# PEER with gathered rows: 1.3 rows per step in front of and during the first range's weights, and fewer chunks of U made early

## The chip, the cores and the metric

One core of a Trainium2 chip. The metric is the device time of one execution in microseconds (us). TensorE (PE) multiplies matrices, VectorE (DVE), ScalarE (ACT) and GpSimd (POOL) work on rows of 128 partitions, SyncE (SP) issues most transfers. Each engine runs its own instructions strictly in the order in which the program has them, and waits by semaphores for the others.

## The reference

Two models run one after the other. The part that the change touches is layer 0 of the first model, where the same PEER layer is applied to two streams of 256 tokens of width 1024, the context xc and the latents x:

```python
def _peer(h, w_q, keys, u_tab, v_tab):
    def block(hb):
        ...
        e = i1 * N_KEYS + i2
        g = jax.nn.softmax(sc.astype(jnp.float32), axis=-1).astype(hb.dtype)
        a = jax.nn.gelu(jnp.einsum('nhkd,nd->nhk', u_tab[e], hb)) * g
        return jnp.einsum('nhk,nhkd->nd', a, v_tab[e])
...
        x = x + mod[5] * _peer(h, *peer_args)
        if not last:
            ...
            xc = xc + modc[5] * _peer(hc, *peer_args)
```

Each token chooses 8 x 16 = 128 of 16384 experts. For each chosen expert e, row e of U is dotted with the token, gelu is applied, the result is weighted by g, and row e of V times that number is added.

## The kernel before

`peer0` computes the layer for both streams at once, in two different ways.

*The context is gathered.* `gathered` is a generator that yields after each row. A "row" here is a tile of 128 x 1024 f32, 512 KB, which POOL fetches with one indirect DMA (`rows_of`, L1394): for one token its 128 rows of V, or for 128 tokens one row of U each. First come 256 rows of U; VectorE dots each with the tokens (L1409, into `dots`). After each 128, gelu and weights follow. Then come 256 rows of V, one for each token; TensorE multiplies each with eight small products into `ps_gv`. After every 32 rows ScalarE copies the result (`yg`, L1435), TensorE transposes it (`ps_gT`), and VectorE adds it to the stream's state `XC` (L1443, L1444). The buffers for rows are four quarters of one tile `gb`, and two more (`ht`) once U's rows are done.

*The latents are dense.* All 16384 experts are computed in 128 chunks of 128. `first()` (L1476) loads one chunk of U (512 KB), multiplies (`ps_U`, f32) and puts gelu of it (L1481) into a ring `A` of 52 chunks. `peer_weights` (L1218) makes the factors g of 32 experts' chunks (a range) in 33 steps: VectorE makes P (L1244), P (L1247) and Pg (L1250), TensorE multiplies them (`ps_G`, f16), and `use` (L1232) multiplies the ring's chunks with the result. `second(c)` (L1483) splits the ring's chunk into a high and a low part (`a_hi` L363 on ACT, `a_lo` L364 on DVE), loads a chunk of V, splits that too (`whi` L350, `wlo` L353) and adds twelve products to `ps_acc`. After chunk 127 `peer_out` copies `ps_acc` to `y`, transposes it (`ps_yT`) and adds it to X (L1571). The next stage begins with the sums of squares of XC and X (`sq` L523 and L540, POOL's additions `R` L527, `ps_ss`), the reciprocal `R` (L555) and the projection `ps_in`.

*What sets the order.* `units(n)` (L1470) adds n to a credit and takes one row from the generator for each whole credit. It is called in the front of the context (`fc`), in the front of x (`fx`, 46 steps), once per `first()` in the steps of range 1's weights (`gens[0]`), and then with 2.1 (`UNITS`) after each `second` and each `first`. Rows that are left when the loop ends are taken at its end, before the stage closes. `first()` is called in the fronts under a condition on the step's number; what the ring of 52 then lacks (`more`) is spread over the 33 steps of the first range. A scheduler reorders instructions within what dependences and buffers allow, so that an instruction's place on its engine can be ahead of its place in the program.

Of the kernel before, what the change touches and what calls it, by code (L numbers as in the profile page):

```python
# [297 lines left out]
class Kern:  # L298
# [1153 lines left out]
    def peer0(self, side=()):  # L1452


        nc = self.nc
        es = ExitStack()
        self.ctx_done = False
        self.peer_open(es, 1, self.RANGES0)
        pe = self.pe
        self.keys = pe.tile([P, 2, P], FT, name="keys")  # L1460
        nc.sync.dma_start(self.keys, self.A["keys0"].rearrange("p (q e) -> p q e", q=2))
        sc, sx = {}, {}
        self.gather_open(sc)
        R = self.RING0
        A = pe.tile([P, R, NT], FT, name="A")
        pos = {"u": 0, "v": 0}
        credit = [0.0]
        gath = self.gathered(sc)

        def units(n=None):  # L1470
            credit[0] += self.UNITS if n is None else n
            while credit[0] >= 1 and not self.ctx_done:
                next(gath)
                credit[0] -= 1

        def first():  # L1476
            c = pos["u"]
            pos["u"] += 1
            ps = self.psb("ps_U")[:, :NT]
            self.lin_32(self.load_w(self.A["U0"][c]), sx["h"], ps)  # L1480
            nc.scalar.activation(A[:, c % R], ps, AF.Gelu_apprx_tanh)  # L1481

        def second(c):  # L1483
            t = A[:, c % R]
            a = (pe.tile([P, NT], FR, tag="a_hi", bufs=2, name="a_hi"),
                 pe.tile([P, NT], FR, tag="a_lo", bufs=2, name="a_lo"))
            self.hilo(a[0], a[1], t)
            w = self.weight(self.A["V0"][c])
            for b in range(2):
                bs = slice(b * P, (b + 1) * P)  # L1490
                for n in range(2):
                    ns = slice(n * 512, (n + 1) * 512)
                    self.mm3(acc[2 * b + n], (a[0][:, bs], a[1][:, bs]), (w[0][:, ns], w[1][:, ns]), c == 0, c == P - 1)

        def ahead():
            return pos["u"] < P and pos["u"] < pos["v"] + R and sx.get("h") is not None

        fc, fx = self.peer_front(0, 0, sc, True), self.peer_front(0, 1, sx)
        self.pool_each = 1 << 30
        next(fc)  # L1500
        while "h" not in sx:
            next(fx)
            next(fc)
        for k, _ in enumerate(fc):
            if (k > 24 or k % 4 == 3) and ahead():
                first()
            if "blocks" in sc:
                units(1)
        for k, _ in enumerate(fx):
            if (k > 32 or k % 2) and ahead():  # L1510
                first()
            units(self.UNITS / 2)
        ranges, i0 = [], 0
        for n in self.RANGES0:
            ranges.append((i0, n))
            i0 += n
        gens = [self.peer_weights(sx, A, i0 % R, i0, n) for i0, n in ranges]
        side = [f(pe) for f in side]
        NB = NT // self.TB + 1
        more = R - pos["u"]  # L1520
        for k, _ in enumerate(gens[0]):
            for _ in range((k + 1) * more // NB - k * more // NB):
                first()
                units()
        nr, left = 1, NB
        for c in range(P):
            pos["v"] = c
            if c == 0:
                acc = [self.psa("ps_acc") for _ in range(4)]
            if nr < len(ranges):  # L1530
                i0, n = ranges[nr]
                if pos["u"] >= i0 + n:
                    k = -(-left // max(1, i0 - c - 1))
                    for _ in range(min(k, left)):
                        next(gens[nr])
                        left -= 1
                    if left == 0:
                        nr, left = nr + 1, NB
            second(c)
            units()  # L1540
            pos["v"] = c + 1
            if ahead():
                first()
                units()
            if not self.ctx_done:
                self.advance(side)
            if c == P - 1:
                self.peer_out(0, 1, acc)
        for _ in gath:
            pass  # L1550
        self.advance(side, 1000)
        self.pool_each = 4
        es.close()
# [803 lines left out]
```

## Time and profile before

| | |
|---|---|
| median of 3 runs | 4083.49 us (4080.9 to 4084.05) |
| profiled execution | 4071.07 us |
| its span | 4069.2 us |
| granted TensorE clock, mean | 0.961 of full speed |
| TensorE busy | 3736.2 us (92%) |
| VectorE busy | 2718.9 us (67%) |
| ScalarE, GpSimd busy | 1522.1 us, 1333.6 us |
| U rows dotted (L1409) | 256 x 1.22 us |

The stage of `peer0` that matters here lies between 867 and 1984 us of the span. The table of stretches below gives, for each stretch, its length, then for each engine the busy time with the number of instructions in brackets, the granted clock of TensorE (1.00 is full speed, 0.50 half), the busy share of the 16 DMA engines and the GB/s they moved. Timeline rows have the start, the duration of a run of like instructions, the engine, the line, the operation, out<-in, and in square brackets the idle time of the engine before them with what ended it. A tile's view lists how long and how often the engine of an instruction on that tile stood idle before it, by what ended that.

### The profile page before, as it was taken

To read this page: it belongs to the slowest core of one execution; us is meant where nothing else is said; L and a number is where in the kernel's file an instruction comes from. 1 tells how busy PE (TensorE), PEld (TensorE's weight loads), DVE (VectorE), ACT (ScalarE), POOL (GpSimd) and SP (SyncE) were. 2 spreads that over 40 slices of the span, in tenths; PEclk is the share of its full clock that TensorE was granted. 3 is DMA by queue.
4 is the path that set the end of the run, shared out by engine and by line. 5 is a ranking of instruction groups with operands and counts; after the bars stand their busy time and mean duration, and the time that the engine had idled before them with its cause. 6 is when DMAs were issued, how large, how long until landed. Compare 5 with 4: busy or idle time off the path is not lost. (4 is left out here: it accounts for less than half of the span.)

```text
span 4069.2 us, 69007 instructions
## 1 busy us (share of the span) xinstructions
PE 3736.2 (92%) x26811; PEld 3164.7 (78%) x26811; DVE 2718.9 (67%) x5739; ACT 1522.1 (37%) x2552; POOL 1333.6 (33%) x916
## 2 busy tenths in 40 slices
PE   8999996866898889999799988999999999999999
PEld 6777875755676666666589988889778899999999
DVE  5833368788787642374585799886785666864785
ACT  6433320111121211233455443444334646553554
POOL 0022205432435434455314456322442131231122
PEclk9999997987898999999899999999999999999999
DMA  5254238965989889999545544556446413565355
GB/s 211 70 166 140 79 119 281 334 218 192 355 306 365 333 312 354 336 353 403 194 130 163 160 146 126 160 168 191 150 146 189 144 48 113 178 198 179 92 178 151
DMA packets 228952, 827.48 MB, mean 203 GB/s; under 512 B 25736, under 2 KB 27408, under 8 KB 228624
## 3 DMA queue, kind: packets, MB, share of 16 engines
q1 hardware_dynamic: 154752, 554.08, 42.2%
q0 software_dynamic: 73728, 268.47, 17.8%
q8 instruction: 211, 3.46, 0.3%
q14 instruction: 117, 0.96, 0.1%
q10 hardware_dynamic: 144, 0.52, 0.0%
HBM read 821.91 MB, written 1.06 MB: 202 GB/s over the span
## 5 line engine op out<-in xcount | busy, mean ns | idle before, releaser
L350 ACT CAST whi<-raw 128x1024 fp32r<-128x1024 f32 (+1 forms) x774 | 802.0, 1039 | 975.8 <-DMA raw<-in_V 322.0
L353 POOL TENSOR_TENSOR wlo<-raw,whi 128x1024 fp32r<-128x1024 f32 (+1 forms) x230 | 570.6, 2482 | 1457.8 <-ACT whi L350 1308.5
L353 DVE TENSOR_TENSOR wlo<-raw,whi 128x1024 fp32r<-128x1024 f32 (+1 forms) x544 | 670.2, 1233 | 459.8 <-ACT whi L350 454.6
L1394 POOL DMA_INDIRECT gb<-in_Ur,er x256 | 329.6, 1288 | 536.0 <-DVE gb L1409 300.3
L323 PE MATMUL ps_U<-h,raw 128*128 128x256 f32 x2048 | 483.1, 392 | 23.9 <-ACT A L1481 23.7
L323 PEld LDWEIGHTS ps_U<-h,raw 128*128 128x128 f32 x2048 | 398.5, 197 | 93.7 <-ACT A L1481 24.6
L323 PE MATMUL ps_acc<-wlo,a_hi 128*128 128x512 f32 x1024 | 420.6, 411 | 46.2 <-DVE wlo L353 43.7
L323 PE MATMUL ps_acc<-whi,a_hi 128*128 128x512 f32 x1024 | 430.2, 424 | 15.4 <-ACT whi L350 15.4
L323 PE MATMUL ps_acc<-whi,a_lo 128*128 128x512 f32 x1024 | 415.7, 406 | 0.0
L1409 DVE SCALAR_TENSOR_TENSOR gb<-gb,ht 128x1024 f32<-128x1024 f32 x256 | 310.2, 1223 | 124.3 <-DMA gb<-in_Ur,er 123.1
L363 ACT CAST a_hi<-A 128x256 fp32r<-128x256 f32 x256 | 103.5, 405 | 568.4 <-PE ps_acc L323 525.5
L323 PE MATMUL ps_U<-h_hi,whi 128*128 128x256 f32 x1024 | 294.3, 287 | 7.9 <-DVE A L1232 5.4
L323 PE MATMUL ps_U<-h_hi,wlo 128*128 128x256 f32 x1024 | 291.4, 285 | 8.4 <-DVE wlo L353 6.5
L323 PE MATMUL ps_U<-h_lo,whi 128*128 128x256 f32 x1024 | 290.8, 284 | 0.0
L323 PEld LDWEIGHTS ps_acc<-wlo,a_hi 128*128 128x128 f32 x1024 | 200.5, 196 | 95.3 <-DVE wlo L353 53.3
L323 PE MATMUL ps_in<-hh_hi,whi 128*128 128x256 f32 (+1 forms) x776 | 265.9, 345 | 1.7 <-ACT hh_hi L568 1.7
L323 PE MATMUL ps_in<-hh_hi,wlo 128*128 128x256 f32 (+1 forms) x776 | 262.3, 339 | 1.1 <-POOL wlo L353 1.1
L323 PEld LDWEIGHTS ps_acc<-whi,a_hi 128*128 128x128 f32 x1024 | 198.6, 195 | 83.0 <-ACT whi L350 20.7
L323 PE MATMUL ps_in<-hh_lo,whi 128*128 128x256 f32 (+1 forms) x776 | 262.9, 340 | 0.0
L364 DVE TENSOR_TENSOR a_lo<-A,a_hi 128x256 fp32r<-128x256 f32 x256 | 117.5, 460 | 201.8 <-ACT a_hi L363 199.7
L1394 POOL DMA_INDIRECT gb<-in_V,eT x170 | 182.5, 1073 | 178.0 <-PE ps_gv L323 145.4
L323 PEld LDWEIGHTS ps_acc<-whi,a_lo 128*128 128x128 f32 x1024 | 200.6, 196 | 47.6 <-DVE a_lo L364 0.6
(636 smaller groups left out, 8748.9 us busy)
## 6 DMA issues: line engine op xcount, KB each, us to landing
raw<-in_U SPq DMA_DIRECT2D x256, 512.0 KB, 4.3
raw<-in_V SPq DMA_DIRECT2D x256, 512.0 KB, 4.5
raw<-in_win SPq DMA_DIRECT2D x96, 512.0 KB, 3.8
raw<-in_wup SPq DMA_DIRECT2D x88, 512.0 KB, 3.8
raw<-in_wada SPq DMA_DIRECT2D x80, 512.0 KB, 4.8
raw<-in_wq SPq DMA_DIRECT2D x48, 512.0 KB, 4.5
raw<-in_gwin SPq DMA_DIRECT2D x37, 512.0 KB, 3.7
raw<-in_wdn SPq DMA_DIRECT2D x32, 512.0 KB, 4.1
```

Of the source, the lines that this page charges most:

```text
L323: self.nc.tensor.matmul(o, l, r, start=start, stop=stop)
L350: nc.scalar.copy(hi[:, :f], raw[:, :f])
L353: eng.tensor_sub(lo[:, :f], raw[:, :f], hi[:, :f].bitcast(FT))
L363: (copy or self.nc.scalar.copy)(hi, src)
L364: self.nc.vector.tensor_sub(lo, src, hi.bitcast(FT))
L1394: self.nc.gpsimd.indirect_dma_start(t, None, table, bass.IndirectOffsetOnAxis(ap=at, axis=0), bounds_check=P * P - 1, oob_is_err=False)
L1409: nc.vector.scalar_tensor_tensor(t, t, 1.0, st["ht"][:, b], op0=OP.mult, op1=OP.mult, accum_out=st["d"][:, b, j:j + 1])
```

## The change

Two loops of `peer0` are changed, three lines in all.

```diff
         for k, _ in enumerate(fx):
-            if (k > 32 or k % 2) and ahead():
+            if k % 2 and ahead():
                 first()
-            units(self.UNITS / 2)
+            units(1.3)
...
         for k, _ in enumerate(gens[0]):
             for _ in range((k + 1) * more // NB - k * more // NB):
                 first()
-                units()
+            units(1.3)
```

In the front of x, `first()` is called at odd steps alone, where before it was called at every step after the 32nd; 23 chunks of U are made there instead of 29, 44 in both fronts instead of 50, and 8 of the ring's 52 instead of 2 are left for range 1's weights. The credit is 1.3 per step there instead of 1.05. In the 33 steps of range 1's weights it is 1.3 per step, in place of 2.1 per chunk of U. By the program's credits 110 rows instead of 60 are taken when chunk 0 of V begins.

VectorE in the middle of range 1's weights. Before, each step is four rows long: P of the step (L1244, L1247), the use of the step ahead (L1232), the step's two Pg (L1250).

```order
L1232 SCALAR_TENSOR_TENSOR A<-A,ps_G 128x32x8
L1250 TENSOR_TENSOR Pg<-P_6513,gT 128x256 x2
L1244 TENSOR_TENSOR P_6539<-io_t,i2T 128x1024
L1247 TENSOR_TENSOR P_6541<-io_t,i1T 128x256
L1232 SCALAR_TENSOR_TENSOR A<-A,ps_G 128x32x8
```

The same place in the changed kernel:

```order
L1250 TENSOR_TENSOR Pg<-P_6501,gT 128x256 x2
L1232 SCALAR_TENSOR_TENSOR A<-A,ps_G 128x32x8
L1244 TENSOR_TENSOR P_6531<-io_t,i2T 128x1024
L1250 TENSOR_TENSOR Pg<-P_6533,gT 128x256 x2
L1247 TENSOR_TENSOR P_6569<-io_t,i1T 128x256
L1247 TENSOR_TENSOR P_6601<-io_t,i1T 128x256
L1409 SCALAR_TENSOR_TENSOR gb,dots<-gb,ht 128x1024 x2
L1232 SCALAR_TENSOR_TENSOR A<-A,ps_G 128x32x8
```

Two rows (L1409) and the next steps' P stand ahead of a use now, because on TensorE a chunk of U (`ps_U`) stands between the products for the weights after every fourth step; before, this happened once in the 33 steps.

VectorE near chunk 21 of V, while range 2's weights are made. Before:

```order
L353 TENSOR_TENSOR wlo<-raw,whi 128x1024
L1247 TENSOR_TENSOR P_8782<-io_t,i1T 128x256
L1247 TENSOR_TENSOR P_8811<-io_t,i1T 128x256
L364 TENSOR_TENSOR a_lo<-A,a_hi 128x256
L1409 SCALAR_TENSOR_TENSOR gb,dots<-gb,ht 128x1024 x2
L442 TENSOR_TENSOR adar<-adar,ps_ada 128x256
L1232 SCALAR_TENSOR_TENSOR A<-A,ps_G 128x20x8
L1232 SCALAR_TENSOR_TENSOR A<-A,ps_G 128x12x8
L1244 TENSOR_TENSOR P_8780<-io_t,i2T 128x1024
```

The same place in the changed kernel:

```order
L364 TENSOR_TENSOR a_lo<-A,a_hi 128x256
L353 TENSOR_TENSOR wlo<-raw,whi 128x1024
L1409 SCALAR_TENSOR_TENSOR gb,dots<-gb,ht 128x1024 x4
L1244 TENSOR_TENSOR P_9097<-io_t,i2T 128x1024
L1247 TENSOR_TENSOR P_9099<-io_t,i1T 128x256
L1232 SCALAR_TENSOR_TENSOR A<-A,ps_G 128x20x8
L1250 TENSOR_TENSOR Pg<-P_9099,gT 128x256 x2
L1232 SCALAR_TENSOR_TENSOR A<-A,ps_G 128x12x8
```

Four rows stand between two chunks there instead of two.

TensorE at the stage's end, from the last product into `ps_acc`. Before, the products of the context's rows (`ps_gv`) go on among the transposes of x's result (`ps_yT`) and behind them:

```order
L323 MATMUL ps_acc<-whi,a_lo 128x512
L323 MATMUL ps_gv<-gb,Z_3988 32x256 x8
L328 MATMUL ps_yT<-cst,y 128x128 x6
L323 MATMUL ps_gv<-gb,Z_3989 32x256
L328 MATMUL ps_yT<-cst,y 128x128 x4
L323 MATMUL ps_gv<-gb,Z_3989 32x256 x4
```

The changed kernel:

```order
L323 MATMUL ps_acc<-whi,a_lo 128x512
L328 MATMUL ps_yT<-cst,y 128x128 x16
L323 MATMUL ps_ss<-R,ones 128x256
L323 MATMUL ps_ss<-sq,ones 128x256 x8
L323 MATMUL ps_in<-hh_hi,whi 128x256 x3
```

The last product of a row stands twelve chunks of V before this, and ScalarE's squares of XC and POOL's additions of them, which stood behind the last row, stand ahead of the last chunks too.

## Rows read from the trace of the kernel before

**Rows 1.** Busy time by stretch, all engines; the first row names the columns.

```profile
core 0: us, PE busy (x) PEld busy (x) DVE busy (x) ACT busy (x) POOL busy (x), PEclk, DMA share, GB/s
867.00:916.00 49.00, 36.61 (x157) 30.89 (x158) 49.00 (x160) 9.36 (x20) 6.09 (x4) 0.83 0.37 119
916.00:972.00 56.00, 30.56 (x531) 23.54 (x528) 53.43 (x165) 3.37 (x7) 2.58 (x3) 0.61 0.20 71
972.00:1094.00 122.00, 99.16 (x467) 74.87 (x466) 84.27 (x149) 22.38 (x42) 67.00 (x52) 0.89 0.96 356
1094.00:1232.00 138.00, 130.38 (x1035) 103.53 (x1036) 121.27 (x307) 28.75 (x53) 49.78 (x38) 0.96 0.88 314
1232.00:1391.00 159.00, 129.33 (x610) 98.26 (x609) 109.71 (x200) 29.63 (x52) 83.17 (x65) 0.87 0.98 369
...
1793.00:1935.00 142.00, 141.78 (x1021) 91.89 (x1018) 61.59 (x93) 48.17 (x74) 76.92 (x73) 1.00 1.02 401
1935.00:1984.00 49.00, 31.27 (x242) 11.11 (x235) 8.73 (x22) 10.30 (x24) 28.39 (x30) 0.69 0.76 290
```

**Rows 2.** The same stretches, instructions of line 364 (a_lo, one per chunk) alone.

```profile
1793.00:1935.00 142.00, 14.05 (x33) 1.00 1.02 401
```

**Rows 3.** Timeline of TensorE in range 1's weights.

```profile
938.32 0.76 PE L323 MATMUL ps_G<-Pg,P 128*128 128x32 f16 x16 [0.78 <-DVE Pg L1250]
...
944.47 5.26 PE L323 MATMUL ps_U<-h,raw 128*128 128x256 f32 x14
```

**Rows 4.** Timeline of VectorE at the same place.

```profile
940.73 0.41 DVE L1232 SCALAR_TENSOR_TENSOR A<-A,ps_G 128x256 f32<-128x256 f32 x1
...
942.27 0.41 DVE L1232 SCALAR_TENSOR_TENSOR A<-A,ps_G 128x256 f32<-128x256 f32 x1
...
944.67 0.42 DVE L1232 SCALAR_TENSOR_TENSOR A<-A,ps_G 128x256 f32<-128x256 f32 x1 [0.17 <-PE ps_G L323]
...
950.16 0.42 DVE L1232 SCALAR_TENSOR_TENSOR A<-A,ps_G 128x256 f32<-128x256 f32 x1 [1.38 <-PE ps_G L323]
```

**Rows 5.** Tile gb, 984 to 1090: dots, idle before them, landing of DMAs.

```profile
L1409 DVE SCALAR_TENSOR_TENSOR gb<-gb,ht x44: 1209/1225/1278, 983.8 to 1089.4; 128x1024 f32<-128x1024 f32 x44
...
  DMA gb<-in_Ur,er: 31.5, 20
...
DMA to landing us min/median/max: 5.0/7.4/11.0
```

**Rows 6.** Tile gb, 1090 to 1225.

```profile
  DMA gb<-in_Ur,er: 7.8, 4
...
DMA to landing us min/median/max: 4.9/6.2/10.0
```

**Rows 7.** Timeline of TensorE at the stage's end.

```profile
1923.93 0.50 PE L323 MATMUL ps_acc<-whi,a_hi 128*128 128x512 f32 x1
...
1926.88 1.07 PE L323 MATMUL ps_gv<-gb,Z 128*32 128x256 f32 x16
...
1934.53 0.39 PE L323 MATMUL ps_acc<-whi,a_lo 128*128 128x512 f32 x1
...
1967.75 1.08 PE L323 MATMUL ps_gv<-gb,Z 128*32 128x256 f32 x8 [0.17 <-DMA gb<-in_V,eT]
...
1978.77 1.22 PE L323 MATMUL ps_ss<-R,ones 128*128 128x256 f32 x2 [8.76 <-POOL R L527]
...
1983.66 0.47 PE L323 MATMUL ps_in<-hh_hi,whi 128*128 128x256 f32 x1
```

**Rows 8.** Timeline of VectorE at the stage's end.

```profile
1941.12 0.48 DVE L1571 SCALAR_TENSOR_TENSOR X<-ps_yT,mods,X 128x256 f32<-128x256 f32 x1 [1.36 <-PE ps_yT L328]
...
1970.45 0.48 DVE L1444 TENSOR_TENSOR XC<-XC,rg 128x128 f32<-128x128 f32 x2
```

**Rows 9.** The page's costliest groups: busy, mean ns, idle before and its releaser.

```profile
L1394 POOL DMA_INDIRECT gb<-in_Ur,er x256 | 329.6, 1288 | 536.0 <-DVE gb L1409 300.3
...
L1409 DVE SCALAR_TENSOR_TENSOR gb<-gb,ht 128x1024 f32<-128x1024 f32 x256 | 310.2, 1223 | 124.3 <-DMA gb<-in_Ur,er 123.1
```

## The prediction

> **What bounds the kernel now.** I read the table by stretches first [rows 1], cut where the loop over V's chunks starts chunk 0 (972), 14 (1094), 30 (1232), 46 (1391) and 94 (1793) and where it ends (1935); chunks are counted by a_lo, and in the last of these stretches 33 of its 34 have a record [rows 2]. The next stage needs both streams, so the stretches lie one behind the other, and a change in one moves the end by its own amount. In each I ask which column is full. While the weights of range 1 are made (916 to 972), VectorE is busy 53.43 of 56 us and the DMA share is 0.20. In chunks 0 to 14 and again in 30 to 46 the DMA is full (0.96 and 0.98) and VectorE is idle for 38 and 49 us. In chunks 14 to 30 no column is full, but three are near: TensorE 130.38 of 138, VectorE 121.27, DMA 0.88. From 1793 to 1935 TensorE is full (141.78 of 142). The last stretch, 1935 to 1984, is the odd one: TensorE 31.27 of 49 us at clock 0.69. The chain at the end [rows 7, 8] says why: the last product of x's stream starts at 1934.53, but rows of V are still being fetched and multiplied until 1967.75, each of the late ones after a wait for its DMA; then XC is updated, squared and summed, and the next stage's first product starts at 1983.66. From the first late row's product (1934.85) to there are 48.8 us, and x's own share of it ends with X at 1941.6.
>
> So rows are the currency. All 512 must be paid somewhere; the tail pays 1.25 us for each of its last rows (1.08 of products and 0.17 of wait [rows 7], some 20 such rows). The question is what they cost where the change puts them.
>
> **What the change moves.** Rows dotted on VectorE, counted in the two programs' orders: at the start of range 1's weights 100 and 100 (the scheduler had already taken rows ahead of the program's credits, so 1.3 for 1.05 in the front does nothing), at their end 105 and 115, at chunk 14 157 and 169, at chunk 30 195 and 236. U's rows end near chunk 46 and near chunk 36. Rows of V multiplied by chunk 64 are 73 and 123, by chunk 94 160 and 211. In the changed order the last row stands 12 chunks before the last chunk. So the added rows lie: +10 in range 1's weights, +2 in chunks 0 to 14, +29 in chunks 14 to 30, +6 in 30 to 46, +3 in 46 to 64, none in 64 to 94; taken away are 24 to 26 in the last 12 chunks and 24 in the tail. Eight chunks of U, not two, are left for the weights' time.
>
> **A, the weights of range 1.** Ten rows at 1.22 us [rows 9] on an engine that is full: +12.2. Seven chunks of U stand between the groups of products for the weights instead of one. What one costs is seen at 944: the products of a chunk take 5.26 us at the low clock [rows 3], and VectorE's next use waits 0.17 and 1.38 us although a cast's remainder and a row filled the gap [rows 4]. Per interval of four steps TensorE then needs 4 x 0.76 + 5.2 = 8.2 us, VectorE 4 x 1.54 (the distance of two uses in the quiet part) + 1.4 rows x 1.22 = 7.9, against 6.2 for VectorE before: some 2 us for each of seven intervals, rows included, so +14. Bounds: +10 (the rows use VectorE's 2.6 us of idle and no product is waited for) and +23 (seven times the 1.55 us of waits come on top of the rows). The chunks of U come out of the front before 916, where VectorE is busy 49.00 of 49.00: nothing is gained there, as TensorE's 36.61 hid them. The granted clock is 0.61 in this stretch, and products ran at half speed. The Trainium skill, "TensorE: Matmul & The Clock Gate", Part 1, says that the throttled state is the default and that activity releases it; by that the seven chunks could lift the clock here, and A would be the rows alone, 12 in place of 14. No row here shows which.
>
> **B, chunks 0 to 14.** Two rows; the DMA is full and a row waits 31.5/44 = 0.72 us for landing [rows 5], so 2 x (1.22 + 0.72) at most: +3 (0 to 4).
>
> **C, chunks 14 to 30 with range 2's weights.** This is the largest term and the least certain. VectorE gets 29 x 1.22 = 35.4 us more: 121.3 + 35.4 = 156.7 us of work in a stretch of 138. If its idle time closes wholly, the stretch grows by 19; if the 16.7 us of idle that it has now stay, by 35. I take the middle, +27, since VectorE at 95% beside the same chain of steps is what range 1's weights show. The DMA agrees: 138 us at 314 GB/s are 43.3 MB, 29 rows of 128 x 1024 x 4 bytes add 15.2, and 58.5 MB at 369 GB/s, the rate of the full stretch behind, are 159 us (+21), at the 401 GB/s of chunks 94 to 128 146 us (+8). So VectorE binds, not the DMA. The Trainium skill, "HBM Reference", Specifications, gives about 358 GB/s as one core's share and about 425 for a core that streams alone. By the first the DMA would need 163 us here (+25), by the second 138 (nothing); the trace, with 401 GB/s over 142 us, agrees with the second, and the sum goes without both.
>
> **D and E.** Chunks 30 to 46 are full in DMA: 6 rows are 3.1 MB, at 369 GB/s +8 (0 to 10). In 46 to 64 three rows of V more, 0.53 us each on TensorE (two take 1.07 [rows 7]), +2 (0 to 4). Behind that to chunk 94 the same number of rows in both.
>
> **H, chunks 94 to 128.** Of 34 chunks in 142 us, 4.18 us each, the last 12 lose their two rows. Between the start of the chunk at 1923.93 and the rows behind it at 1926.88 lie 2.95 us [rows 7], which is a chunk without rows. VectorE is busy 61.59 and ScalarE 48.17 of the stretch's 142 us [rows 1], so neither takes TensorE's place. 12 x (4.18 - 2.95) = -15 (-12 to -16).
>
> **Tail.** With the rows gone, behind the last chunk stand the 16 transposes, X's update and the sums of squares. Before, the first took 1934.85 to 1941.6 with pieces of rows between; without those (some 3 us) 4 are left. The sums and the first hh took 1978.77 to 1983.66, 4.9 us at the low clock. So 9 to 10 are left of 48.8: -39 (-36 to -41). Squares of XC, POOL's additions and XC's update are queued ahead of the last chunks in the changed order, under TensorE's full time, and cost nothing as long as chunks last: if that cover were gone, the 8.76 us in which the sums of squares waited for POOL [rows 7] would come back.
>
> **The sum.** 14 + 3 + 27 + 8 + 2 = +54; 15 + 39 = -54. The change moves some 50 rows from places where one costs 1.1 us (54 for 50) to places where one costs 1.1 us. Net 0: the profiled execution's 4071.07 us stays, and so does the median, 12.4 us above it, 4083.5. All times below are on the median's side.
>
> **Rivals.**
> *Slower: landing waits come to chunks 14 to 30.* There are four buffers for rows of U. One is away for issue 1.3 [rows 9], landing 6.2 [rows 6] and the dot 1.2, 8.7 us; four of them give a row each 2.2 us, so the stretch's 38 + 29 = 67 rows need 146 us of its 165. It holds, but with a landing of 7.4, the median of the stretch before with its full DMA [rows 5], it is 166, and beyond that the buffers bind. The changed order puts rows in bursts of four in front of the next step of the weights, so VectorE would stand, and with it TensorE. Price: 29 x 0.72 = +21, total 4104. For it: the DMA share would be about 0.95 there. Against: the rows waited only 7.8 us for landing in 36 in that stretch [rows 6].
> *Faster: rows fill what is idle.* A is +10, B 0 (VectorE's idle 38 us take them and the DMA has 4% left), C +19, D and E 0 if the DMA runs at 401 instead of 369 GB/s: +29 - 54 = -25, total 4058. For it: VectorE was busy 49.00 of 49.00 in the front, so it can be filled wholly when rows are at hand. Against: in 916 to 972 it was not.
> *The change does not do what it says:* the scheduler had taken rows ahead already, so credits would change nothing, 4083.5. The orders speak against it: rows at chunk 30 differ by 41.
>
> **How the numbers follow.** A measurement of this kernel can tell about 0.2%, 8 us, from no change. The even exchange has 0.50, with its own range 4068 to 4098 from C alone at its ends (-8, +8) and A's and D's; of that 0.34 lies within 8 us, 0.08 on each side. The landing wait has 0.22, slower. The idle filling has 0.25, faster. No effect has 0.03, same. Faster 0.33, same 0.37, slower 0.30. The range from 4058 to 4107 leaves out half of each outer case, about 0.2.
>
> **What would show it.** In the changed profile: the stretch between the first P and the first a_hi should be near 70 us (before 56); chunks 14 to 30 near 165 us with VectorE at 95% or more; the last 12 chunks about 3 us each; and from the last product of x's stream to the next stage's first product about 10 us with no row between. The landing wait would show as idle time of VectorE before rows released by the DMA, over 20 us in chunks 14 to 30. The prediction is wrong if the tail keeps a wait other than for rows, or if chunks 14 to 30 grow by less than 19 us.

## The result, and the profile after

The changed kernel takes 4114.95 us (median of 4 runs, 4107.54 to 4122.13) against 4082.19 us: the ratio is 1.0082, with a 95% interval of 1.0062 to 1.0102. It is slower by some 33 us, and it lies above the range that was given. The profiled execution took 4113.93 us.

The table of stretches for the changed kernel, cut at the starts of chunks 0, 14, 30, 46, 64, 76, 94 and 127. ([rows 1] has its cut for chunk 14 some 4 us early, and its last cut not at the start of chunk 127 but at its last product.) Columns: length, busy time of PE, PEld, DVE, ACT, POOL with counts, granted clock, DMA share, GB/s.

```profile
918.00:990.00 72.00, 52.70 (x622) 43.55 (x619) 64.44 (x184) 4.42 (x13) 13.07 (x13) 0.86 0.47 157
990.00:1114.00 124.00, 100.89 (x474) 75.98 (x473) 86.58 (x157) 23.96 (x45) 67.42 (x53) 0.89 0.96 357
1114.00:1296.00 182.00, 145.46 (x1046) 109.50 (x1045) 150.57 (x350) 30.39 (x53) 84.83 (x66) 0.91 0.91 325
1296.00:1462.00 166.00, 143.74 (x913) 99.83 (x912) 64.52 (x127) 29.32 (x55) 72.65 (x65) 0.91 0.93 346
1462.00:1660.00 198.00, 182.70 (x1718) 130.27 (x1711) 87.64 (x234) 32.96 (x59) 79.73 (x78) 0.97 0.91 335
1660.00:1791.00 131.00, 107.22 (x716) 72.45 (x714) 22.66 (x39) 21.24 (x40) 50.34 (x49) 0.90 0.83 297
...
1888.00:2011.00 123.00, 122.05 (x812) 84.05 (x811) 57.90 (x82) 49.47 (x79) 53.43 (x51) 1.00 0.90 337
2011.00:2027.00 16.00, 15.64 (x86) 12.54 (x86) 13.27 (x26) 10.57 (x22) 3.40 (x3) 1.00 0.70 229
```

The third row is the news: chunks 14 to 30 take 182 us, and in them neither VectorE (150.57) nor TensorE (145.46) nor the DMA (0.91) is full. The last row is what the change was good for: it has 16 us in place of the tail's 49 [rows 1], and the first 5 of them are chunk 127's own products.

Timed by the start of each chunk's cast a_hi in the trace, the stretches compare as follows. The first trace of the kernel before was a short execution (4071 us beside a median of 4082), so a second one (4082.07 us) was taken; it stands in the second column and is what the changes are reckoned against.

| stretch | before, 1st | before, 2nd | after | forecast | measured |
|---|---|---|---|---|---|
| first P to chunk 0 (A) | 80.0 | 79.4 | 97.3 | +14 | +17.9 |
| chunks 0 to 14 (B) | 126.4 | 125.7 | 122.6 | +3 | -3.1 |
| 14 to 30 (C) | 133.2 | 131.3 | 182.1 | +27 | +50.8 |
| 30 to 46 (D) | 161.0 | 162.0 | 166.0 | +8 | +4.0 |
| 46 to 64 (E) | 186.9 | 187.5 | 198.6 | +2 | +11.1 |
| 64 to 76 | 115.8 | 125.5 | 130.9 | 0 | +5.4 |
| 76 to 94 | 96.5 | 96.5 | 97.3 | 0 | +0.8 |
| 94 to 127 (H) | 134.7 | 134.3 | 122.3 | -15 | -12.0 |
| 127 to the next stage's first product | 56.9 | 58.2 | 12.7 | -39 | -45.5 |

The sum of the last column is +29.4. The two gains came nearly as forecast, 57.5 us together for 54; cut at the last product of chunk 127, as the forecast cut them, chunks 94 to 127 gave back 14.6 and the tail 42.9. C alone took 24 us more than its term.

What VectorE waited for in C, from the view of the tile gb of the changed kernel, 1114 to 1296; it answers to [rows 6]:

```profile
L1409 DVE SCALAR_TENSOR_TENSOR gb<-gb,ht x65: 1207/1220/1227, 1116.3 to 1294.6; 128x1024 f32<-128x1024 f32 x65
...
  DMA gb<-in_Ur,er: 22.5, 20
...
DMA to landing us min/median/max: 4.4/7.7/11.0
```

The same view of the kernel before, in its chunks 14 to 30 (1098 to 1232; [rows 6] begins at 1090 and takes in waits of chunk 13):

```profile
  DMA gb<-in_Ur,er: 2.1, 1
...
DMA to landing us min/median/max: 4.9/6.2/8.8
```

And the busy times of that stretch in the second trace of the kernel before:

```profile
1099.00:1230.30 131.30, 125.92 (x1025) 99.89 (x1024) 116.53 (x294) 28.54 (x52) 47.64 (x36) 0.97 0.89 317
```

Twenty times VectorE stood before a row that had not landed, 22.5 us in all; before, it was once, 2.1 us. VectorE's busy time grew from 116.53 to 150.57 us, by 34 (28 rows more), and the landing waits by 20. These 54 us are more than C's 50.8, as VectorE's other idle time fell from 13 to 9 us. TensorE's busy time grew as well, from 125.92 to 145.46 us for nearly as many products, at a granted clock of 0.91 instead of 0.97; but of VectorE's idle time only 4.2 us were waits for TensorE, so the stretch goes by VectorE's own chain. And who stood behind VectorE, from the list of waits in the same stretch (in total, times, longest):

```profile
PE ps_G L323 <- DVE Pg L1250: 28.5, 17, 7.1
...
DVE gb L1409 <- DMA gb<-in_Ur,er: 22.5, 20, 4.1
```

TensorE waited 28.5 us for the factors Pg, which stand behind the rows on VectorE. In the kernel before there is no such wait in that stretch.

The end of the stage, timeline of TensorE, which answers to [rows 7]:

```profile
2016.03 0.39 PE L323 MATMUL ps_acc<-whi,a_lo 128*128 128x512 f32 x1
2016.26 1.21 PE L328 MATMUL ps_yT<-cst,y 128*128 128x128 f32 x8
2017.79 1.52 PE L328 MATMUL ps_yT<-cst,y 128*128 128x128 f32 x8 [0.32 <-DVE X L1571]
2019.35 0.67 PE L323 MATMUL ps_ss<-R,ones 128*128 128x256 f32 x2
2019.86 3.62 PE L323 MATMUL ps_ss<-sq,ones 128*128 128x256 f32 x16
2023.44 0.62 PE L323 MATMUL ps_in<-hh_hi,whi 128*128 128x256 f32 x3
```

From the last product to the next stage's first lie 7.4 us, with TensorE at full clock and never long idle.

### The profile page after: what moved, and what is told of

Read it like the earlier page. It is cut to its first block, busy times and chain, and to the rows that moved or that the text cites. A ratio compares the mean times of both kernels' runs of the same rounds, so it can differ in the third digit from the quotient of the medians.

```text
span 4112.1 us, 68984 instructions
## 1 busy us (share of the span) xinstructions
PE 3741.4 (91%) x26811; PEld 3172.5 (77%) x26811; DVE 2711.8 (66%) x5739; ACT 1519.5 (37%) x2551; POOL 1323.8 (32%) x916
## 5 line engine op out<-in xcount | busy, mean ns | idle before, releaser
L323 PE MATMUL ps_U<-h,raw 128*128 128x256 f32 x2048 | 513.2, 405 | 5.4 <-DMA raw<-in_U 2.9
L323 PE MATMUL ps_acc<-whi,a_hi 128*128 128x512 f32 x1024 | 417.5, 420 | 20.1 <-ACT whi L350 20.0
L1409 DVE SCALAR_TENSOR_TENSOR gb<-gb,ht 128x1024 f32<-128x1024 f32 x256 | 309.6, 1222 | 123.4 <-DMA gb<-in_Ur,er 122.5
L323 PE MATMUL ps_U<-h_hi,wlo 128*128 128x256 f32 x1024 | 292.0, 285 | 10.2 <-DVE wlo L353 8.3
```

The source lines that it names most:

```text
L323: self.nc.tensor.matmul(o, l, r, start=start, stop=stop)
L1409: nc.vector.scalar_tensor_tensor(t, t, 1.0, st["ht"][:, b], op0=OP.mult, op1=OP.mult, accum_out=st["d"][:, b, j:j + 1])
```

## The experiments

The theory with which they began: C grew by VectorE's work for the rows (34 us) and by waits for rows to land (20 us), since there are four buffers. A grew because of the chunks of U. The stretches 46 to 76 were open.

### The two parts of the change apart

*Credits alone* (the old condition for U, two chunks left):

```diff
-            if k % 2 and ahead():
+            if (k > 32 or k % 2) and ahead():
```

> The changed kernel with the old condition for U (two chunks left for range 1's weights, not eight); the credits of 1.3 stay. By the order 110 rows instead of 116 are done at chunk 0, and from chunk 14 on the row counts are those of the changed kernel. Theory: the stretch of range 1's weights grew by 17 us because seven chunks of U stand in it; here it falls back to about +5 us over the kernel before (4 rows), chunks 0 to 14 take six rows more and grow by about 7, and the total stays within 8 us of the changed kernel, near 4110. Rival: the 10 rows cost that time themselves; then the stretch of the weights keeps about +12 us and the total does not move.

Measured: 4117.03 us, ratio 1.0074 (1.0054 to 1.0095). A took 83.5 us, four over the kernel before, with four rows more; chunks 0 to 14 took 128.6 us with 53 rows, and 14 to 30 191.8 with 69. The theory holds for A; the rows that A no longer took were paid in the two stretches behind it.

*U alone* (the kernel before with the new condition, and credits of 4.2 over the 33 steps, so that no row is asked for earlier):

```diff
-            if (k > 32 or k % 2) and ahead():
+            if k % 2 and ahead():
...
-                units()
+            units(4.2 / NB)
```

> The kernel before with the new condition for U alone: eight chunks are left for range 1's weights, the credits stay (1.05 per step in front, 4.2 over the 33 steps of the weights). By the order the scheduler fills the gaps with rows: 114 at chunk 0 (before 106), but from chunk 30 on it is within 8 of the kernel before, and the tail keeps its 26 rows. Theory: range 1's weights grow by about 15 us as in the changed kernel, chunks 14 to 30 stay near 134 us, the tail stays near 57 us; 8 rows fewer in chunks 30 to 46 give back up to 10 us. Total 4085 to 4100. Rival: the chunks of U cost nothing, only the rows do; then the total stays within 5 us of the kernel before, because the eight early rows are given back one for one.

Measured: 4106.92 us, ratio 1.0053 (1.0035 to 1.0070), above what was expected. A took 100.1 us, the tail 59.1. So leaving eight chunks of U costs 20 us in A together with the eight rows with which the scheduler filled the gaps; the rows' share is 8 x 1.22 = 10 us of VectorE's work. Only 7 us of it come back, in chunks 30 to 46 (154.4 for 53 rows instead of 162.0 for 62). Chunks 14 to 30, 46 to 64 and 76 to 94 took 4 to 6 us more each for the same rows or one more; why stays open. A's stretch in this kernel:

```profile
919.00:995.50 76.50, 55.33 (x642) 45.66 (x640) 65.37 (x187) 5.58 (x13) 12.91 (x12) 0.84 0.45 151
```

VectorE is busy 65.37 of 76.5 us; in [rows 1] it was 53.43 of 56. Work was added and, nearly as much, idle time.

### Fewer rows in chunks 14 to 30

```diff
-            units()
+            units(1.2 if 14 <= c < 30 else self.UNITS)
```

(and the same behind `first()`)

> The changed kernel with 1.2 credits in place of 2.1 while chunks 14 to 30 run, which leaves 38 rows there instead of 67; 29 rows move behind, and 4 are left for the tail. Theory: the 49 us that chunks 14 to 30 took more are 35 us of VectorE work and 20 us of waits for rows to land, both only because 65 rows stand there; the stretch falls from 182 to 133-140 us, the last 12 chunks take back 12 to 15 us and the tail 5; total about 4088. Rival (the forecast's reading): the rows cost 1.0 us each there, the landing waits would be in the stretch with fewer rows as well; then it falls to about 155 us only and the total to about 4105.

Measured: 4085.01 us, ratio 1.0005 (0.9994 to 1.0015). The stretch fell from 182.1 to 133.0 us; 38 rows of U were dotted in it, and in the tile's view no landing wait is left. The 27 rows that moved were paid again at the end, +14 us in 94 to 127 and +15.5 in the tail; chunks 30 to 76, with nearly as many rows as in the changed kernel (187 and 189), took 20 us less, 13 of them at a wait that a later experiment takes up (11.1 us instead of 23.8). The theory's number for C was right. The stretch:

```profile
1118.00:1251.00 133.00, 127.71 (x1024) 100.08 (x1023) 118.37 (x298) 28.94 (x52) 48.60 (x39) 0.97 0.91 332
```

So 27 rows (65 - 38) had cost 49 us in C, 1.8 us each, which is more than in the tail (1.25).

### Rows two at a time instead of four

The credits of chunks 14 to 30 are given with the steps of the weights (`busy` is true for a chunk in which steps of range 2's weights are made):

```diff
                     for _ in range(k):
                         next(gens[nr])
+                        units(2 * self.UNITS / k if nr == 1 else 0)
...
-            units()
+            units(0 if busy else None)
```

> The changed kernel with the same number of rows in chunks 14 to 30, but given step by step of range 2's weights, two at a time, instead of four at once behind each chunk. Theory: the landing waits come from bursts of four rows on four buffers; with bursts of two VectorE's idle time before rows falls from 22.5 us to under 8 and the stretch from 182 to about 163 us, total about 4096. Rival: 67 rows on four buffers, each away for 9 to 10 us, need 160 us or more however they are placed; then the waits stay above 15 us and the stretch above 175 us.

Measured: 4116.67 us, ratio 1.0079 (1.0062 to 1.0095); the stretch took 181.7 us. In the trace 32 of the 37 groups of rows now have one or two rows and three have four, where the changed kernel has 14 groups of four, and still:

```profile
  DMA gb<-in_Ur,er: 19.9, 15
```

The theory in this form fell: not the bursts make the wait. 66 rows in 182 us are 2.76 us each, 11.0 us for one turn of each of four buffers. In the changed kernel's trace, with issues, landings and dots paired in their order, a turn in C takes 11.1 us on the mean: 7.4 from the start of the issue to the landing, 1.5 until VectorE begins the dot, 1.2 for the dot, 0.9 to the next issue into that buffer. In the kernel before (second trace) it takes 14.3, and 5.7 of them the landed row lies waiting for VectorE: there the buffers are not what is short. The rival was right: in this placement, too, so many rows do not go through four buffers faster.

### A fifth buffer

A fifth row takes 4 KB per partition. Here they come from the ring, which has 48 chunks instead of 52; a control has that ring and four buffers.

```diff
-    RING0 = 52
+    RING0 = 48
...
-        st["buf"] += [t[:, i] for i in range(4)]
+        st["buf"] += [t[:, i] for i in range(4)] + [self.pe.tile([P, D], FT, name="gb5")[:, :]]
```

> The changed kernel with a ring of 48 chunks instead of 52 (four chunks of U less ahead); the control for the next kernel. Rows at chunk 14 and 30 by the order: 166 and 236 (169 and 236). Both theories: chunks 14 to 30 stay near 182 us with some 20 us of landing waits.

> The same with a fifth buffer for rows in the memory that the ring gave up. Theory: the four buffers bind (66 rows in 182 us are 2.76 us each, 11.0 us for a buffer's turn); with five a row needs 2.2 us, VectorE's work of 157 us binds instead, and chunks 14 to 30 fall to 160-165 us with under 8 us of landing waits. Rival: the DMA is what limits; then landing takes longer by as much, and the stretch stays above 175 us.

Measured, one execution each: 4134.78 us with four buffers, 4077.2 with five. The stretch of chunks 14 to 30 of the two, four buffers first:

```profile
1118.00:1303.50 185.50, 151.25 (x1048) 112.83 (x1046) 149.93 (x344) 30.07 (x52) 89.53 (x68) 0.89 0.89 322
```

```profile
1083.00:1253.00 170.00, 142.25 (x1039) 107.24 (x1038) 144.50 (x339) 30.04 (x52) 89.10 (x63) 0.93 0.92 341
```

185.4 us became 170.0, the landing waits 21.9 became 9.8 us. Four rows fewer stand in the stretch with five buffers (62 for 66), which is 5 us of the 15 at a dot's 1.22; the rest goes with the landing waits. The rival's number, above 175 us, did not come, and the DMA moved 341 GB/s instead of 322, so it had not been at its end. The gain was smaller than expected in this stretch, and larger outside: the front ended 22 us sooner (first P at 876.5 instead of 899.0), chunks 0 to 14 took 118.9 instead of 128.4 us. The price of the smaller ring was seen beside it: chunks 76 to 94 took 122 us in both, against 97 with the ring of 52.

Then the memory was found without the ring: the two tiles `y` of `peer_out` take a part of the tile that h32 had used.

```diff
-                ys = [pe.tile([P, 512], FT, tag="y", bufs=2, name="y") for _ in range(2)]
+                t = self.in_hh(0, "y", FT)
+                ys = [t[:, b, 0:2].rearrange("p k n -> p (k n)") for b in range(2)]
```

In the changed kernel:

> The changed kernel, ring of 52 as it was, with a fifth buffer for rows (its memory is that of the two tiles y, which take a part of the tile h32 at the end). Theory: front 15-20 us shorter, chunks 0 to 14 9 us, chunks 14 to 30 15 to 20 us shorter, as between the two kernels with the ring of 48: total 4055 to 4070. Rival: a part of that gain was the ring's (fewer chunks of U in the weights); then the total stays above 4080.

Measured: 4068.72 us, ratio 0.9959 (0.9945 to 0.9973). Against the changed kernel the front is 18 us shorter, A 3, chunks 0 to 14 7 and 14 to 30 17 us (165.3), with 61 rows in them instead of 65:

```profile
1085.00:1250.50 165.50, 141.21 (x1048) 107.01 (x1047) 145.46 (x344) 29.93 (x52) 81.75 (x61) 0.93 0.92 340
```

```profile
  DMA gb<-in_Ur,er: 8.8, 8
...
DMA to landing us min/median/max: 4.9/8.1/10.9
```

A landing took a little longer than with four buffers (8.1 us for 7.7), and yet the waits for it fell from 22.5 to 8.8 us. So the fifth buffer turns the change's loss into a small gain. But what is left of the change itself is told by the same buffer in the kernel before:

> The kernel before with the fifth buffer and nothing else. Theory: the front gains the same 15-20 us, chunks 0 to 14 5 to 9 us, chunks 14 to 30 nothing (37 rows don't wait for buffers there), the tail keeps its 57 us: total 4055 to 4065, so that the change to the credits is worth nothing with five buffers either, or a little. Rival: without the many rows of the changed kernel the buffers bind nowhere; total within 5 us of the kernel before.

Measured: 4048.86 us, ratio 0.9916 (0.9899 to 0.9932), better than the changed kernel with five. The front gained 9 us, A 3, chunks 0 to 14 8, while 14 to 30 lost 7 (138.1 with 38 rows). So with five buffers the change lengthens C by 27.2 us for 23 rows more, 1.2 us each, as much as a dot takes; with four it was 50.8 us for 28, 1.8 each. The difference is what the lack of a buffer cost. The largest gain is where none was expected, in chunks 30 to 46: 144.6 us with 56 rows, where four buffers took 162.0 with 62 and, in the kernel with U alone, 154.4 with 53:

```profile
1217.00:1361.50 144.50, 125.09 (x608) 94.19 (x607) 101.12 (x186) 30.04 (x53) 76.51 (x59) 0.93 0.98 382
```

The DMA share is 0.98 as in [rows 1], but 382 GB/s went through instead of 369. A stretch that the forecast had called full of DMA waited for the four buffers too. The tile's view there, of the kernel before and with five buffers:

```profile
  DMA gb<-in_Ur,er: 39.8, 27
...
DMA to landing us min/median/max: 4.6/7.2/9.4
```

```profile
  DMA gb<-in_Ur,er: 12.9, 16
...
DMA to landing us min/median/max: 5.9/8.5/11.3
```

But here the landing itself rose from 7.2 to 8.5 us with the fifth buffer, where in C it rose by 0.4; and six rows fewer are a part of the gain.

### The transposes of a finished group

In chunks 64 to 76 TensorE waits for one thing only. The list of its waits there, of the second trace of the kernel before and of the changed kernel:

```profile
PE ps_gT L328 <- ACT yg L1435: 16.3, 1, 16.3
```

```profile
PE ps_gT L328 <- ACT yg L1435: 23.8, 2, 14.7
```

The copy yg of a finished group of 32 rows stands on ScalarE behind the cast of a chunk of V, as the timeline of ScalarE in the changed kernel shows:

```profile
1680.92 1.05 ACT L350 CAST whi<-raw 128x1024 fp32r<-128x1024 f32 x1 [10.45 <-DMA raw<-in_V]
...
1691.02 1.04 ACT L350 CAST whi<-raw 128x1024 fp32r<-128x1024 f32 x1 [8.48 <-DMA raw<-in_V]
...
1698.14 1.04 ACT L350 CAST whi<-raw 128x1024 fp32r<-128x1024 f32 x1 [5.50 <-DMA raw<-in_V]
1699.09 0.36 ACT L1435 COPY yg<-ps_gv 128x256 f32<-128x256 f32 x1
```

TensorE's transposes of yg stand among the twelve products for the chunk that was cast at 1680.92: five of them have run when TensorE stops (14.7 us), the other seven wait, and with them the buffers that the next chunks of V need. Two casts of V later the copy has its turn. The experiment moves the transposes and XC's update (`add`) eight rows later:

```diff
-            pt = self.psb("ps_gT")
-            ...
+            late = (g, y)
...
+                if k == 7 and late:
+                    add(*late)
```

> The changed kernel, but the two transposes of a finished group of 32 rows and XC's update come eight rows later in the program, not directly behind the copy of the group's result. Theory: in chunks 64 to 76 TensorE waits 23.8 us at these transposes alone (14.7 and 9.1), because the copy on ScalarE stands behind the cast of the chunk of V after the one whose products are ready; with other work between, the gaps go, the stretch falls from 131 to about 110-115 us and the total to about 4098. Rival: TensorE waits for V's transfers, and the transposes are only where that shows; then the wait moves to the products of a chunk, the stretch stays above 125 us and the total within 5 us of the changed kernel.

Measured: 4102.02 us, ratio 1.0036 (1.0018 to 1.0053), against 1.0082 without it. The waits are gone:

```profile
PE ps_U L323 <- ACT A L1488: 4.0, 2, 3.1
...
PE ps_gT L328 <- ACT yg L1449: 0.3, 1, 0.3
```

Chunks 64 to 76 took 126.7 us with 54 rows, after 130.9 with 48, and 76 to 94 90.5 with 38 instead of 97.3 with 42: 11 us together, where 16 to 20 were expected. The stretch stayed above 125 us, as the rival had it; but the total fell by 0.46% of the kernel before, some 19 us, where the rival allowed 5. The wait was a real one, not only another name for the DMA's, but a part of it came back.

### Rows moved from the tail to the end of the loop

The kernel before with 2.8 credits in place of 2.1 from chunk 76 on:

```diff
-            units()
+            units(self.UNITS if c < 76 else 2.8)
```

> The kernel before, with 2.8 credits in place of 2.1 from chunk 76 of V on; nothing else is changed. By the order 51 rows instead of 37 stand in chunks 76 to 94, 82 instead of 70 behind, none in the tail. Theory: the rows that the tail pays with 1.25 us each and its fixed 13 us chain are cheaper here: 14 rows at 0.53 us of TensorE in 76 to 94 and 12 to 16 at 1.3 us (the DMA at 401 GB/s) behind, +7 and +18, against -44 for the tail: total about 4063 to 4068. Rival: the DMA is at its end in both stretches, a row costs 1.3 us everywhere; then +37 - 44, total 4072 to 4080.

Measured: 4078.01 us, ratio 0.9985 (0.9973 to 0.9998): the rival's number. The tail fell from 58.2 to 14.7 us, but chunks 76 to 94 took 105.1 us instead of 96.5 for 11 rows more, and 94 to 127 163.8 instead of 134.3 for 19 rows more, 1.55 us each. In the changed kernel the same stretch gave back only 12 us for 20 rows fewer, 0.6 each. So a row beyond some two a chunk cost more than in the tail. What sets that price is not shown:

```profile
1806.00:1970.00 164.00, 155.76 (x1125) 87.20 (x1124) 58.18 (x87) 45.92 (x70) 89.30 (x84) 0.99 0.99 384
```

The DMA share is 0.99, but it moved less than the 402 GB/s of the kernel before (second trace), and TensorE is busy 155.76 of 164 us.

### The kernel before once more

> The kernel before once more, for a second trace: how far the same stretches differ from one execution to the next. If the first trace was a lucky one (its 4071 us lie under the median), the stretches with a full DMA (chunks 46 to 76) come out some 10 us longer, and the gap at the transposes near chunk 71 nearer to 15 us than to 9; else all stretches repeat within 3 us.

Measured: 4082.07 us. All stretches repeat within 2 us but one: 64 to 76 took 125.5 us, the first time 115.8, and the wait at the group end in it 16.3 us instead of 8.7. So 10 us of what looked like the changed kernel's loss in the first comparison belong to the first trace.

### What was learnt, put together

The changed kernel with the fifth buffer, the later transposes, and other credits:

```diff
-            units()
+            units(1.5 if 14 <= c < 30 else 2.1 if c < 76 else 2.4)
```

> The changed kernel with the fifth buffer, the transposes of a group eight rows later, and 1.5 credits in place of 2.1 while chunks 14 to 30 run, 2.4 from chunk 76 on. By the order 46 rows in chunks 14 to 30, none in the tail. If the readings add up: 4115 - 22 (front) - 9 (chunks 0 to 14) - 38 (14 to 30) - 10 (transposes) + 15 (19 rows later) = about 4050. If the DMA is the limit behind chunk 30, the 19 rows cost 25 us and the total is about 4060.

Measured: 4033.88 us, ratio 0.9882 (0.9863 to 0.9901), 1.2% faster than the kernel before and better than the sum. Its stretches 14 to 30, 30 to 46 and the tail:

```profile
1088.00:1221.00 133.00, 126.50 (x1026) 98.56 (x1025) 119.85 (x294) 28.52 (x51) 53.94 (x41) 1.00 0.92 336
1221.00:1371.00 150.00, 130.42 (x782) 94.53 (x780) 86.15 (x161) 29.59 (x54) 79.11 (x68) 0.97 1.01 397
...
1925.00:1938.00 13.00, 12.64 (x61) 9.60 (x60) 10.19 (x20) 9.28 (x19) 3.41 (x3) 1.00 0.67 222
```

The first has 43 rows and no excess over the kernel before; the second does 64 rows in 150 us at 397 GB/s, where four buffers took 162 for 62 (22 of the 64 are rows of V, which need no dot); the tail is gone. A kept its loss (93 us), as the eight chunks of U are still there.

## Why the prediction was wrong, point by point

**The step that failed is C.** The forecast set +27 between the bounds 19 and 35, both from VectorE's work and its idle time now, and put waits for landing at nothing in that sum; it kept them as a rival with chance 0.22 and +21 us. VectorE's work was right: +34 us for the 35.4 of the term. Its idle time was wrong: half of the 16.7 us was to close, and it rose to 31, of which 22.5 are landing waits (2.1 before). With the rival's price the term would be 27 + 21 = 48, and +50.8 was measured. The rival's arithmetic stood in the prediction: four buffers with a landing of 6.2 us need 146 us for 67 rows, with 7.4 us 166. The error was to take the landing time of the stretch as it was, with 38 rows in it. With 65 rows the median landing rose to 7.7 us, past the point from which the rival decides. The turn in that arithmetic was not right either: the landing is counted from the start of the issue, so the issue's 1.3 us are in it twice, and the wait of a landed row for VectorE (1.5 us) and the time to the next issue (0.9) are left out. With 7.7 the sum gives 10.2 us, where 11.1 were measured.

**The counter-check did not bear on this.** "The DMA agrees" compared bytes with rates. That asks whether the DMA can carry the rows, not whether four buffers can hold those that are under way. And the rate of the stretch behind, 369 GB/s, was no ceiling: with a fifth buffer the same stretch went at 382, in the combined kernel at 397.

**A** was +17.9 for +14, with the right cause: rows and chunks of U. From the first P (at 892, not at 916, where the forecast's cut lies) to chunk 0 VectorE is busy 88.81 of 97 us, in the second trace before 76.88 of 79: 12 us of work, the ten rows, and 6 of idle time. The credits alone cost 4 us, the chunks of U, with the eight rows that came with them, 20. The granted clock of the stretch rose from 0.61 to 0.86; with the credits alone it was 0.58, with the chunks alone 0.84. With this the trace agrees with the rule of the Trainium skill, "TensorE: Matmul & The Clock Gate", Part 1, that activity releases the throttled state. But A did not become the rows alone: U's products still stand ahead of the next products for the weights, and VectorE waited 7.2 us for those, 2.3 before.

**B and D** were +3 and +8, and came as -3.1 and +4.0. B had 51 rows in both kernels by the trace, where the order's count had two more; D had 64 for 62, not six more.

**E** was +2 and came as +11.1. By the trace 77 rows were done between the casts of chunks 46 and 64, where the kernel before did 64; the orders had shown 76 and 73. The count was made at VectorE's a_lo and TensorE's products, which need not be reached at one time: in the kernel before TensorE's rows lag nine behind the order's place at chunk 64 (320 by the trace, 329 by the order). All kernels with 73 to 79 rows there took 194 to 204 us, those with 64 187 to 192; so the time goes with the rows, at 0.7 to 1.6 us each. No run moved rows in this stretch alone, so this cause is argued, not shown.

**64 to 76** was 0 and came as +5.4, with two group ends instead of one and 23.8 us of waits at them instead of 16.3; the forecast had not counted them. **H** came as worked out (-14.6 for -15 by the forecast's own cut), the **tail** a little better than its range (-42.9 for -39, at most -41). The rival on the other side (rows fill idle time) was wrong in every stretch but B.

The cause that the forecast named for a loss was thus right and its chance too low; the rows' price of 1.1 us, the same on both sides, was an average that hid 1.8 us in the one place to which most of them went.

## What to carry to other kernels

Before more items are sent through a stretch, count the turn of one buffer (from its issue to the landing, the wait for the engine, the use, the time to the next issue) and divide by the number of buffers: that is a rate like an engine's, and it binds while no engine is full. Take the landing time that the stretch will have with the added transfers, not the one it has; and where a DMA share near 1 stands beside waits for landing, try one buffer more before calling the bytes the limit. A small copy that opens or closes a group should not stand in an in-order queue behind a cast that waits for a transfer, if another engine's whole queue stands behind that copy.

## What the runs showed of the hardware

The DMA share does not tell how much more could go through: 0.98 stood beside 369 GB/s with four buffers and beside 382 with five, and 1.01 beside 397. The highest rate over a long stretch was 402 GB/s (1.02, chunks 94 to 127 of the second trace before); asking for 19 more rows there cost 1.55 us each, and the rate fell to 384. A row of 512 KB landed 6.2 us (median) after its issue in chunks 14 to 30 of the kernel before, 7.7 in the changed kernel with 1.8 times as many rows, and 8.1 there with a fifth buffer. Two executions of the same program differed by 10 us in one stretch of 12 chunks and by under 2 us in all others.
